# A decoder layer on one core: each gate's two 16-bit parts become one 32-bit word in the one-hot product, with four one-hot buffers and new gather rates

## The chip, the cores and the metric

The kernel runs on one core of a Trainium2 chip. The metric is device time in microseconds, from launch to end. Before the change three runs took 1726.3 to 1732.9 us, with a median of 1727.87 us. The profile is of one further execution.

The core's engines run side by side, each through its own list of instructions in fixed order, and wait for each other by semaphores: PE (TensorE, matmuls; PEld is its loading of weights), DVE (VectorE), ACT (ScalarE), POOL (GpSimd, which here issues the indirect DMAs that gather rows) and SP (SyncE, which issues the other DMAs). Sixteen DMA engines move the data between HBM and the on-chip memory.

## The reference, cut to what matters

The layer is one inference step for 512 prompt tokens and 64 sample tokens with the same weights: a projection, windowed attention and a spatial gating unit side by side, a merge, then a mixer over single-neuron experts (PEER), then a per-layer embedding. The change is in the mixer:

```python
q = (xb @ w_q).reshape(blk, PEER_HEADS, 2, PEER_HALF)
sc = jnp.einsum('thcd,hcnd->thcn', q, sub_keys)
s_top, i_top = lax.top_k(sc, PEER_TOPK)
...
best, pos = lax.top_k(cand, PEER_TOPK)
idx = jnp.take_along_axis(cand_idx, pos, axis=-1)
gate = jax.nn.softmax(best, axis=-1)
u = expert_u[idx]
act = jax.nn.gelu(jnp.einsum('thkd,td->thk', u, xb))
w = gate * act
return jnp.einsum('thk,thkd->td', w, expert_v[idx])
```

Each token takes 8 heads x 16 = 128 of the 16384 experts. An expert's number is i x 128 + j, with i from the first list of keys and j from the second.

## The kernel before, in words

**Two ways through the mixer.** 192 tokens (the 64 sample tokens and the first 128 prompt tokens, "tile" 0 and 1) are done by gathering: for each of 64 + 128 slots GpSimd fetches one row of `peer_u` per partition (L724, one indirect DMA of 128 rows of 4 KB), DVE forms the dot products (L736); then as many rows of `peer_v` are fetched and DVE adds them, weighted, to an accumulator (L743). That makes 192 + 192 row gathers, with five row buffers. The other 384 tokens (three tiles) are done densely over all experts, in blocks of 128 experts with the same j:

- *Stage 1* (`stage1`, 128 blocks): load a block of `peer_u` (512 KB), split it into a high and a low part (ACT L70, DVE L71 `w_lo`), 24 matmuls of 384 columns (`tform`, L86), GELU on ACT (L794). Each result is kept on chip, or spilled to HBM and read back.
- *G* (`build_g`): the gates as a dense matrix, for 16 tokens per call, 24 calls. For a token with chosen pairs (i, j) and gates g, G[i, j] is the sum of onehot(i) x (g onehot(j)) over its 128 choices, so a matmul of two one-hot matrices per token makes it. It goes to HBM (`gd`, 1 MB per call) and is read back by blocks.
- *Stage 2* (`stage2`, 128 blocks): multiply a block's activations by its part of G (DVE L1067), split the product and a block of `peer_v`, 18 matmuls of 512 columns (L1028) into six accumulators.

**How G is made before the change.** `make_ew` turns the lists of a tile so that the 128 choices lie on the partitions: `ij` holds i and j as f16. The gate, times 2^14, is kept as two f16 numbers, a high part and the rest (`g16`), and as the same two numbers in f32 (`gf`). `build_g` goes by groups of four tokens, 96 groups in all. DVE writes the one-hots of i and j for the four tokens in one operation (`hot`, L875, 128x1024 f16). Then onehot(j) is multiplied by both parts of the gate (`og`): in every even group ACT does it with 8 instructions of 128x128, one per token and part, with the gate's column as scale (L881); in every odd group DVE does it with 2 instructions of 128x512 (L887). PE then runs 8 matmuls, one per token and part, the two parts adding up in PSUM (L894), and ACT copies the four results into `gs` (L898). `hot` and `og` have three buffers (`OPB`); `gs` has two; after four groups SP writes `gs` to `gd` (L901).

**What sets the order.** Everything is recorded in program order and a scheduler sorts each engine's list by priorities; G's matmuls have a raised priority (`RUNP`). The program loops over the 24 calls of `build_g`, with as many stage-1 blocks between them as a goal line says; the top-16 selection of the last two tiles (`retrieve`) is worked off in the first seven (`TBK`). After the loop six more stage-1 blocks stand before the second stage. The second stage loops over j = 0 to 127 and runs one remaining stage-1 block at most steps until none are left.

**Gathers by credit.** `pay(x)` adds x to a credit and records one gather step for each whole unit. The rates are: `GT` per call of `build_g` (2.0 in the first seven calls, 3.5 in those behind, none in the last two), `GP` per stage-1 block (0.5 before the loop over G, 0 in it, 1.65 in the second stage), and `G2` per step of the second stage (1.6 while stage-1 blocks are left, 2.0 after that). At j = 122 (`TAIL1`) whatever is left is recorded at once. Before j = 126 the accumulator of the last gathered tile is read for its norm (L1014).

In this document the *middle stage* is the time from 572 us, about when DVE writes the first one-hots, to 852.57 us, when the first matmul of the second stage runs.

Of the kernel before, what the change touches and what calls it, by code (L numbers as in the profile page):

```python
# [18 lines left out]
P = 128  # L19
# [5 lines left out]
NJ = 128  # L25
TB = 16
JB = 8
GP = [0.5, 0.0, 1.65]
G2 = (1.6, 2.0)
SPILL = set(range(2, 40, 2))  # L30
NSP = len(SPILL)
GT = (2.0, 3.5)
GS = 2.0 ** 14
TAIL0 = 112
TAIL1 = 122
S1_TOPK = (4, 9, 13)
TBK = 7
S1_END = 6
OPB = 3
G_LAG = 3  # L40
RUNP = 400
RING = 44
# [9 lines left out]
def tile_decoder_step(ctx: ExitStack, tc: tile.TileContext, a, o):  # L52
    nc = tc.nc
    V, A, T, G, S = nc.vector, nc.scalar, nc.tensor, nc.gpsimd, nc.sync

    def pool(stack, name, bufs, side="left", **kw):
        return stack.enter_context(tc.tile_pool(name=name, bufs=bufs, side=side, reuse_waits="tile", **kw))
# [115 lines left out]
    for k in range(KC):  # L173
        with tc.high_priority(offset=1500):
            A.activation(xn[0][k], xT[k], AF.Copy, scale=vecs[:, k:k + 1])
            V.scalar_tensor_tensor(xn[1][k], xT[k], vecs[:, k:k + 1], xn[0][k].bitcast(F32),
                                   op0=ALU.mult, op1=ALU.subtract)
# [405 lines left out]
        split(xc, xn2[0][:, k, :], xn2[1][:, k, :])  # L583

    TOPK = ((4, 4), (0, 8), (1, 8), (2, 8), (3, 8))
    top = [tk.tile([P, 2, 8, 16], F32, name="top", bufs=5) for _ in TOPK]
    tix = [tk.tile([P, 2, 8, 16], U32, name="tix", bufs=5) for _ in TOPK]
    scs = []

    def key_scores(h, c, qp, sk):  # L590
# [139 lines left out]
    def gather_steps():  # L730
        for ti, ns in ((0, NS), (1, P)):
            dots = gp.tile([P, P], F32, name="dots")
            wts = gp.tile([P, P], F32, name="wts")
            for s in range(ns):
                row_ = gather_row(a["peer_u"], ixs[ti][:, s:s + 1])
                V.scalar_tensor_tensor(row_, row_, 1.0, xrs[ti], op0=ALU.mult, op1=ALU.mult,  # L736
                                       accum_out=dots[:, s:s + 1])
                yield
            A.activation(wts[:, :ns], dots[:, :ns], AF.Gelu_apprx_tanh)
            V.tensor_tensor(wts[:, :ns], wts[:, :ns], gts[ti][:, :ns], op=ALU.mult)  # L740
            for s in range(ns):
                row_ = gather_row(a["peer_v"], ixs[ti][:, s:s + 1])
                V.scalar_tensor_tensor(accs[ti], row_, wts[:, s:s + 1], accs[ti], op0=ALU.mult, op1=ALU.add)  # L743
                yield

    prev = None
# [53 lines left out]
    def make_ew(e0, e1_, gtf):  # L800
        pt = bank("pt")
        for q, src in enumerate((e0, e1_, gtf)):
            T.transpose(out=pt[:, q * P:(q + 1) * P], in_=src, identity=ident)
        ij = ep.tile([P, P // 2, 2, 2], F16, name="ij")
        g16 = ep.tile([P, P // 2, 2, 2], F16, name="g16")
        gf = ep.tile([P, 2, P], F32, name="gf")

        def halves(x):
            return x.rearrange("p (u t) -> p u t", t=2)

        for q in range(2):
            A.activation(ij[:, :, q, :], halves(pt[:, q * P:(q + 1) * P]), AF.Copy)
        A.activation(g16[:, :, 0, :], halves(pt[:, 2 * P:3 * P]), AF.Copy, scale=GS)
        A.activation(halves(gf[:, 0, :]), g16[:, :, 0, :], AF.Copy)
        V.scalar_tensor_tensor(gf[:, 1, :], pt[:, 2 * P:3 * P], GS, gf[:, 0, :], op0=ALU.mult, op1=ALU.subtract)
        A.activation(g16[:, :, 1, :], halves(gf[:, 1, :]), AF.Copy)
        ewT.append((ij, g16, gf))

    found = {}
    tqs.close()  # L820
# [40 lines left out]

    def build_g(tb):
        ti, t0 = divmod(tb * TB, P)
        ij, g16, gf = ewT[ti]
        gs = gsp[(tb + 1) % 2].tile([P, NJ, TB], F32, name="gs")
        for t4 in range(0, TB, 4):
            pt = psB.tile([P, 512], F32, name=("sc", "pt")[t4 // 4 % 2])
            hot = op.tile([P, 2, 2, P, 2], F16, name="hot")
            og = op.tile([P, 8 * P], F16, name="og")
            u0 = (t0 + t4) // 2  # L870

            def wide(x):
                return x.rearrange("p u f t -> p (u f) t")[:, :, None, :].to_broadcast([P, 4, P, 2])

            V.tensor_tensor(hot.rearrange("p u f j t -> p (u f) j t"), iota[:, None].to_broadcast([P, 4, P, 2]),  # L875
                            wide(ij[:, u0:u0 + 2]), op=ALU.is_equal)
            if t4 // 4 % 2 == 0:
                right = og.rearrange("p (t h j) -> p t h j", t=4, h=2)
                for t in range(4):
                    for h in range(2):  # L880
                        last = A.activation(right[:, t, h, :], hot[:, t // 2, 1, :, t % 2], AF.Copy,  # L881
                                            scale=gf[:, h, t0 + t4 + t:t0 + t4 + t + 1])
                pairs = [[(hot[:, t // 2, 0, :, t % 2], right[:, t, h, :]) for h in range(2)] for t in range(4)]
            else:
                right = og.rearrange("p (u h j t) -> p u h j t", u=2, h=2, t=2)
                for u in range(2):
                    last = V.tensor_tensor(right[:, u], hot[:, u, 1:2].to_broadcast([P, 2, P, 2]),  # L887
                                           g16[:, u0 + u][:, :, None, :].to_broadcast([P, 2, P, 2]), op=ALU.mult)
                pairs = [[(hot[:, t // 2, 0, :, t % 2], right[:, t // 2, h, :, t % 2]) for h in range(2)]
                         for t in range(4)]  # L890
            with tc.high_priority(offset=RUNP):
                for t in range(4):
                    for h in range(2):
                        g_last[tb] = T.matmul(pt[:, t * P:(t + 1) * P], lhsT=pairs[t][h][0], rhs=pairs[t][h][1],  # L894
                                              start=h == 0, stop=h == 1)
                        if t == h == 0:
                            after(g_last[tb], last)
                A.activation(gs[:, :, t4:t4 + 4], pt.rearrange("p (t j) -> p j t", t=4), AF.Copy, scale=1.0 / GS)  # L898
        if tb == NB // TB - 1:
            A.activation(g0, gs[:, 0:JB, :], AF.Copy)  # L900
        S.dma_start(gd[:, :, tb].rearrange("c p j t -> p c (j t)"), gs.rearrange("p (c j) t -> p c (j t)", j=JB))  # L901
# [13 lines left out]
    for g_ in (ples, xrs_):  # L915
        for _ in g_:
            pass
    pls.close()
    gs_s = ExitStack()
    ep = pool(gs_s, "ep", 2)  # L920
    op = pool(gs_s, "op", OPB)
# [110 lines left out]
    for j in range(NJ):  # L1032
        for jb in (2, 4) if j == 0 else (j + 4,):
            if jb in SPILL:
                back[jb] = d3.tile([P, NB], F32, name="x1c")
                S.dma_start(back[jb], ad[sorted(SPILL).index(jb)])
        if j and j - 1 not in SPILL and j1 < NJ:
            stage1()
        pay(G2[0] if j1 < NJ else G2[1])
        if j == TAIL0:  # L1040
            aLs.close()
            xds.close()
            spp.append(pool(sps, "spare", 2, "right"))
            gather(max(0, P - done[0]), mark_pe[0])
            pg = gp.tile([P, D], F32, name="xr")
            S.dma_start(pg, a["ple_g"])
            tails.append(gathered(0))
            for t in range(NB // P):
                x1s.append(spp[0].tile([P, D], F32, name="x1r", bufs=3))
                S.dma_start(x1s[t], x1r[t])  # L1050
        if j == TAIL1:
            gather(1000, mark_pe[0])
        if j == NJ - 2:
            tails.append(gathered(1))
        if j % JB == 0:
# [11 lines left out]
        V.tensor_tensor(wfv, wfv, gsl[:, :, j % JB, :], op=ALU.mult)  # L1067
# [158 lines left out]
```

## Time and profile before

| | |
|---|---|
| Median of three runs (lowest, highest) | 1727.87 us (1726.3, 1732.9) |
| The profiled execution's own time | 1727.91 us |
| Its span, first to last instruction | 1726.1 us |
| Mean granted clock of TensorE | 0.991 |
| PE, PEld busy | 1686.8, 1523.5 us |
| DVE, ACT, POOL busy | 1419.7, 843.2, 523.4 us |
| DMA, mean over the span | 266 GB/s, 459.11 MB |

How to read it: times count from the start of the span. In the view of 40 slices each digit is the busy share of a slice of 43 us in tenths. In windows and groups, "x" is a count of instructions, and a granted clock of 1.00 is full speed. The DMA share is the mean busy share of the 16 DMA engines, and can go a little over 1. A row of a group ends with the engine's idle time just before such instructions and what ended it. Matmuls overlap, so the time of one is longer than the distance from one to the next; an instruction of DVE or ACT, too, can begin some tens of ns before the one ahead of it ends. SPq and POOLq are the queues from which DMAs are issued.

### The profile page before, as it was taken

What the parts mean: (1) busy time and instruction counts of PE and PEld (TensorE: products, weight loads), DVE (VectorE), ACT (ScalarE), POOL (GpSimd) and SP (SyncE); (2) the same over time, 40 slices, a digit from 0 to 9 for tenths busy, and PEclk for the clock granted to TensorE, in tenths of its full rate; (3) what the DMA queues carried; (4) which work ended last, traced back from release to release, by engine and by line L of the source; (5) the groups of instructions that cost most, each with busy time, mean ns of one, the idle gap of its engine ahead of it and who ended that gap; (6) DMA issues with size and microseconds to landing.
All of it is one profiled execution on the core that took longest, in us unless ns stands there. A gap on an engine that the chain in (4) does not pass through costs nothing.

```text
span 1726.1 us, 27552 instructions
## 1 busy us (share of the span) xinstructions
PE 1686.8 (98%) x10040; PEld 1523.5 (88%) x10040; DVE 1419.7 (82%) x2788; ACT 843.2 (49%) x1528; POOL 523.4 (30%) x390
## 2 busy tenths in 40 slices
PE   8999999999999999888999999999999999999998
PEld 8988999999988999788888888898889998888877
DVE  7365666569899999999698899989888988999873
ACT  6566442343256899888633333333333333333352
POOL 0000000000001113445164555455544554566400
PEclk9999999999999999999999999999999999999999
DMA  6311222433257788999999999999999999999842
GB/s 236 97 62 50 74 95 100 154 102 97 82 165 265 242 278 292 382 357 358 338 355 356 373 401 411 392 396 390 371 339 349 362 345 322 342 375 374 318 165 79
DMA packets 179480, 459.11 MB, mean 266 GB/s; under 512 B 15505, under 2 KB 78993, under 8 KB 177297
## 3 DMA queue, kind: packets, MB, share of 16 engines
q1 hardware_dynamic: 123760, 255.29, 42.0%
q0 software_dynamic: 55584, 202.07, 31.2%
q8 instruction: 78, 1.28, 0.3%
q14 instruction: 58, 0.47, 0.1%
HBM read 420.67 MB, written 37.36 MB: 265 GB/s over the span
## 4 chain that ended last, share of the span: by engine, by line
PE 83%; DVE 11%; DMA 2%; ACT 2%; issue 1%; SPq 0%; ACTq 0%; DVEq 0%
PE mm L86 38%; PE oacc L1028 31%; PE pv L86 4%; DVE w_lo L71 2%; PE oacc L989 2%; PE sc L86 1%; DVE hot L875 1%; DVE row L736 1%; DMA gd<-gs 1%; PE pt L894 1%; PE mm L989 1%; DVE og L887 1%; PE sc L894 1%; ACT w_hi L70 1%; PE pv L338 1%
## 5 line engine op out<-in xcount | busy, mean ns | idle before, releaser
L70 ACT ACTIVATE w_hi<-w_raw 128x1024 fp32r<-128x1024 f32 x321 | 340.0, 1059 | 366.7 <-PE mm L86 278.7
L724 POOL DMA_INDIRECT row<-peer_u,idx x192 | 252.3, 1314 | 821.4 <-DVE best L641 471.4
L71 DVE TENSOR_TENSOR w_lo<-w_raw,w_hi 128x1024 fp32r<-128x1024 f32 x321 | 391.7, 1220 | 73.0 <-ACT w_hi L70 72.3
L86 PE MATMUL mm<-xd,w_hi 128*128 128x384 f32 x1552 | 407.2, 341 | 0.0
L724 POOL DMA_INDIRECT row<-peer_v,idx x192 | 269.6, 1404 | 237.9 <-DVE acc L743 212.7
L86 PE MATMUL mm<-x,w_hi 128*128 128x320 f32 (+1 forms) x1504 | 308.1, 299 | 0.0
L86 PEld LDWEIGHTS mm<-xd,w_hi 128*128 128x128 f32 x1552 | 286.1, 191 | 6.6 <-issue 0.2
L86 PE MATMUL mm<-xd,w_lo 128*128 128x384 f32 x776 | 263.7, 340 | 0.0
L86 PEld LDWEIGHTS mm<-x,w_hi 128*128 128x128 f32 x1504 | 241.8, 190 | 8.2 <-issue 7.4
L743 DVE SCALAR_TENSOR_TENSOR acc<-row,wts,acc 128x1024 f32<-128x1024 f32 x192 | 245.6, 1279 | 3.9 <-DMA row<-peer_v,idx 3.6
L736 DVE SCALAR_TENSOR_TENSOR row<-row,xr 128x1024 f32<-128x1024 f32 x192 | 232.6, 1218 | 13.3 <-DMA row<-peer_u,idx 13.3
L1028 PE MATMUL oacc<-w_hi,wh 128*128 128x512 f32 x768 | 241.3, 394 | 0.6 <-ACT wh L70 0.6
L1028 PE MATMUL oacc<-w_hi,wl 128*128 128x512 f32 x768 | 241.3, 395 | 0.3 <-DVE wl L71 0.3
L1028 PE MATMUL oacc<-w_lo,wh 128*128 128x512 f32 x768 | 240.8, 394 | 0.0
L86 PE MATMUL mm<-x,w_lo 128*128 128x320 f32 (+1 forms) x752 | 223.1, 297 | 0.0
L1028 PEld LDWEIGHTS oacc<-w_hi,wl 128*128 128x128 f32 x768 | 143.5, 187 | 36.6 <-DVE wl L71 1.2
L1028 PEld LDWEIGHTS oacc<-w_lo,wh 128*128 128x128 f32 x768 | 143.6, 187 | 35.4
L1028 PEld LDWEIGHTS oacc<-w_hi,wh 128*128 128x128 f32 x768 | 142.9, 187 | 30.4 <-ACT wh L70 1.0
L86 PEld LDWEIGHTS mm<-xd,w_lo 128*128 128x128 f32 x776 | 147.9, 191 | 0.1
L86 PEld LDWEIGHTS mm<-x,w_lo 128*128 128x128 f32 x752 | 142.4, 189 | 1.0 <-issue 0.8
L86 PE MATMUL pv<-xd,w_hi 128*128 128x384 f32 x496 | 132.1, 341 | 0.0
L881 ACT ACTIVATE og<-hot,gf 128x128 f16<-128x128 f16 x384 | 121.4, 393 | 4.8 <-DVE hot L875 4.8
(333 smaller groups left out, 2093.4 us busy)
## 6 DMA issues: line engine op xcount, KB each, us to landing
w_raw<-peer_uT SPq DMA_DIRECT2D x128, 512.0 KB, 6.1
w_raw<-peer_v SPq DMA_DIRECT2D x128, 512.0 KB, 6.7
gd<-gs SPq DMA_DIRECT2D x24, 1024.0 KB, 9.3
gs<-gd SPq DMA_DIRECT2D x15, 1536.0 KB, 9.9
w_raw<-w_in SPq DMA_DIRECT2D x30, 512.0 KB, 3.7
w_raw<-peer_wq SPq DMA_DIRECT2D x16, 512.0 KB, 3.6
w_raw<-w_br SPq DMA_DIRECT2D x8, 512.0 KB, 3.6
w_raw<-w_out SPq DMA_DIRECT2D x8, 512.0 KB, 3.5
```

The costliest lines, as they stand in the source:

```text
L70: A.activation(hi, src, AF.Copy)
L71: V.tensor_sub(lo, src, hi.bitcast(F32))
L86: mark_pe[0] = T.matmul(ps, lhsT=w[wi][:, wk + k, :], rhs=x[xi][k], start=i == 0, stop=i == n - 1)
L338: ins = T.matmul(pvs[pr, :], lhsT=vt[:, t0 + j, pr], rhs=pT, start=j == 0, stop=j == nj - 1)
L724: ins = G.indirect_dma_start(out=row_, out_offset=None, in_=table, in_offset=bass.IndirectOffsetOnAxis(ap=ix, axis=0))
L736: V.scalar_tensor_tensor(row_, row_, 1.0, xrs[ti], op0=ALU.mult, op1=ALU.mult, accum_out=dots[:, s:s + 1])
L743: V.scalar_tensor_tensor(accs[ti], row_, wts[:, s:s + 1], accs[ti], op0=ALU.mult, op1=ALU.add)
L875: V.tensor_tensor(hot.rearrange("p u f j t -> p (u f) j t"), iota[:, None].to_broadcast([P, 4, P, 2]), wide(ij[:, u0:u0 + 2]), op=ALU.is_e ...
L881: last = A.activation(right[:, t, h, :], hot[:, t // 2, 1, :, t % 2], AF.Copy, scale=gf[:, h, t0 + t4 + t:t0 + t4 + t + 1])
L894: g_last[tb] = T.matmul(pt[:, t * P:(t + 1) * P], lhsT=pairs[t][h][0], rhs=pairs[t][h][1], start=h == 0, stop=h == 1)
L989: T.matmul(p[:r, :hs.stop - hs.start], lhsT=xi[:, k, :r], rhs=w[k][wi][:, hs], start=k == 0 and xi is xh and wi == 0, stop=k == KC - 1 and ...
L1028: mark_pe[0] = T.matmul(oacc[t][hh], lhsT=wi[:, ts], rhs=vi[:, hh * 512:(hh + 1) * 512], start=j == 0 and last == 0 and vi is vh, stop=j = ...
```

## The change

Three things change.

1. **One word per gate.** `make_ew` writes the gate's high part and the rest side by side as two f16 numbers (`gpk`), the high part in the upper half; it is kept at 2^-14 or above. Read as one f32 number, the pair is multiplied by onehot(j) in a single operation with f32 output (`og`): 1 times the word is the word, 0 times it is 0. PE then reads the product as f16 again, every second element for one part. A group on ACT now takes 4 instructions of 128x128, a group on DVE takes 1 of 128x512. Which engine does a group changes too: in the first seven calls three of four groups go to ACT, behind that two of three. Counted in the built program, ACT has 264 such instructions for 384 and DVE 30 for 96. `make_ew` has three ACT instructions fewer per tile and one DVE instruction more.
2. **Four buffers.** `OPB` is 4. To make room, the top-16 lists of the first three tiles lie in a pool of their own that is closed before G's buffers are opened, and `wts` is computed in place in `dots`.
3. **Rates.** `GT` behind the seventh call is 2.9. `G2` has three values: 1.45 for j below 44, then 1.78 while stage-1 blocks are left, then 2.06.

```diff
-G2 = (1.6, 2.0)
+G2 = (1.45, 1.78, 2.06)
-GT = (2.0, 3.5)
+GT = (2.0, 2.9)
-OPB = 3
+OPB = 4
...
-        for q in range(2):
-            A.activation(ij[:, :, q, :], halves(pt[:, q * P:(q + 1) * P]), AF.Copy)
-        A.activation(g16[:, :, 0, :], halves(pt[:, 2 * P:3 * P]), AF.Copy, scale=GS)
-        A.activation(halves(gf[:, 0, :]), g16[:, :, 0, :], AF.Copy)
-        V.scalar_tensor_tensor(gf[:, 1, :], pt[:, 2 * P:3 * P], GS, gf[:, 0, :], op0=ALU.mult, op1=ALU.subtract)
-        A.activation(g16[:, :, 1, :], halves(gf[:, 1, :]), AF.Copy)
+        gpk = ep.tile([P, P, 2], F16, name="gpk")
+        for q in range(2):
+            A.activation(ij[:, :, q, :], pt[:, q * P:(q + 1) * P].rearrange("p (u t) -> p u t", t=2), AF.Copy)
+        V.tensor_scalar(gpk[:, :, 1], pt[:, 2 * P:3 * P], GS, 1.0 / GS, op0=ALU.mult, op1=ALU.max)
+        V.scalar_tensor_tensor(gpk[:, :, 0], pt[:, 2 * P:3 * P], GS, gpk[:, :, 1], op0=ALU.mult, op1=ALU.subtract)
...
-            og = op.tile([P, 8 * P], F16, name="og")
+            og = op.tile([P, 4, P], F32, name="og")
...
-            if t4 // 4 % 2 == 0:
-                right = og.rearrange("p (t h j) -> p t h j", t=4, h=2)
+            grp = tb * TB // 4 + t4 // 4
+            c = t0 + t4
+            if grp % 4 < 3 if tb < TBK else grp % 3 < 2:
                 for t in range(4):
-                    for h in range(2):
-                        last = A.activation(right[:, t, h, :], hot[:, t // 2, 1, :, t % 2], AF.Copy,
-                                            scale=gf[:, h, t0 + t4 + t:t0 + t4 + t + 1])
+                    last = A.activation(og[:, t, :], hot[:, t // 2, 1, :, t % 2], AF.Copy,
+                                        scale=gate[:, c + t:c + t + 1])
             else:
-                right = og.rearrange("p (u h j t) -> p u h j t", u=2, h=2, t=2)
-                for u in range(2):
-                    last = V.tensor_tensor(right[:, u], hot[:, u, 1:2].to_broadcast([P, 2, P, 2]),
-                                           g16[:, u0 + u][:, :, None, :].to_broadcast([P, 2, P, 2]), op=ALU.mult)
+                last = V.tensor_tensor(og.rearrange("p (u t) j -> p u t j", t=2),
+                                       hot[:, :, 1].rearrange("p u j t -> p u t j"),
+                                       gate[:, c:c + 4].rearrange("p (u t) -> p u t", t=2)[:, :, :, None]
+                                       .to_broadcast([P, 2, 2, P]), op=ALU.mult)
+            right = og.rearrange("p t j -> p (t j)").bitcast(F16).rearrange("p (t j h) -> p t j h", t=4, h=2)
...
-        pay(G2[0] if j1 < NJ else G2[1])
+        pay(G2[0 if j < 44 else 1 if j1 < NJ else 2])
```

What stands where in the built programs differs with it. The list of DVE in the middle stage, before the change, where the second dense tile's preparation ends and its first groups begin (`hot` is a one-hot operation, `og` a gate product, `row,dots` the dot products of a gathered row, `w_lo` the split of a stage-1 block):

```order
1119 L815 SCALAR_TENSOR_TENSOR gf<-pt,gf 128x128
1120 L875 TENSOR_TENSOR hot<-iota,ij 128x1024 x2
1121 L887 TENSOR_TENSOR og<-hot,g_6993 128x512 x2
1122 L736 SCALAR_TENSOR_TENSOR row,dots<-row,xr 128x1024
1123 L71 TENSOR_TENSOR w_lo<-w_raw,w_hi 128x1024
1124 L875 TENSOR_TENSOR hot<-iota,ij 128x1024
1125 L736 SCALAR_TENSOR_TENSOR row,dots<-row,xr 128x1024
1126 L887 TENSOR_TENSOR og<-hot,g_6993 128x512 x2
1127 L736 SCALAR_TENSOR_TENSOR row,dots<-row,xr 128x1024
1128 L875 TENSOR_TENSOR hot<-iota,ij 128x1024 x3
1129 L71 TENSOR_TENSOR w_lo<-w_raw,w_hi 128x1024
1130 L887 TENSOR_TENSOR og<-hot,g_6993 128x512 x2
```

The same place of DVE's list in the changed program, where the preparation has two instructions (`gpk`):

```order
1107 L809 TENSOR_SCALAR gpk<-pt 128x128
1108 L870 TENSOR_TENSOR hot<-iota,ij 128x1024
1109 L810 SCALAR_TENSOR_TENSOR gpk<-pt,gpk 128x128
1110 L737 SCALAR_TENSOR_TENSOR row,dots<-row,xr 128x1024
1111 L870 TENSOR_TENSOR hot<-iota,ij 128x1024
1112 L71 TENSOR_TENSOR w_lo<-w_raw,w_hi 128x1024
1113 L879 TENSOR_TENSOR og<-hot,gpk 128x512
1114 L870 TENSOR_TENSOR hot<-iota,ij 128x1024
1115 L737 SCALAR_TENSOR_TENSOR row,dots<-row,xr 128x1024
1116 L870 TENSOR_TENSOR hot<-iota,ij 128x1024
1117 L737 SCALAR_TENSOR_TENSOR row,dots<-row,xr 128x1024
1118 L879 TENSOR_TENSOR og<-hot,gpk 128x512
```

A pair of products for every second one-hot has become one product for two or three one-hots. Over the whole middle stage DVE's list holds 66 gathered rows between the first and the last one-hot before, and 56 now.

The end of the gathers in DVE's list, before the change (`acc` adds a row of `peer_v`, `wl` and `w_lo` are the splits for one step of the second stage):

```order
1950 L743 SCALAR_TENSOR_TENSOR acc<-row,wts,acc 128x1024
1951 L71 TENSOR_TENSOR wl<-x_5421,wh 128x384
1952 L743 SCALAR_TENSOR_TENSOR acc<-row,wts,acc 128x1024
1953 L71 TENSOR_TENSOR w_lo<-w_raw,w_hi 128x1024
1954 L71 TENSOR_TENSOR wl<-x_5421,wh 128x384
1955 L71 TENSOR_TENSOR w_lo<-w_raw,w_hi 128x1024
```

And in the changed program:

```order
1939 L744 SCALAR_TENSOR_TENSOR acc<-row,dots,acc 128x1024
1940 L71 TENSOR_TENSOR w_lo<-w_raw,w_hi 128x1024
1941 L71 TENSOR_TENSOR wl<-aL,wh 128x384
1942 L71 TENSOR_TENSOR w_lo<-w_raw,w_hi 128x1024
1943 L71 TENSOR_TENSOR wl<-aL,wh 128x384
1944 L71 TENSOR_TENSOR w_lo<-w_raw,w_hi 128x1024
```

The last gather stood seven splits of `peer_v` (`w_lo`) before the end of the second stage, and stands three before it now.

More of the change, by code (lines that the diff above doesn't have):

```diff
@@ L585, in tile_decoder_step @@
     TOPK = ((4, 4), (0, 8), (1, 8), (2, 8), (3, 8))
-    top = [tk.tile([P, 2, 8, 16], F32, name="top", bufs=5) for _ in TOPK]
-    tix = [tk.tile([P, 2, 8, 16], U32, name="tix", bufs=5) for _ in TOPK]
+    tes = ExitStack()
+    te = pool(tes, "te", 1, "right")
+    top = [pl.tile([P, 2, 8, 16], F32, name="top", bufs=n) for pl, n in ((te, 3),) * 3 + ((tk, 2),) * 2]
+    tix = [pl.tile([P, 2, 8, 16], U32, name="tix", bufs=n) for pl, n in ((te, 3),) * 3 + ((tk, 2),) * 2]
     scs = []
@@ L732, in gather_steps @@
             dots = gp.tile([P, P], F32, name="dots")
-            wts = gp.tile([P, P], F32, name="wts")
             for s in range(ns):
@@ L738, in gather_steps @@
                 yield
-            A.activation(wts[:, :ns], dots[:, :ns], AF.Gelu_apprx_tanh)
-            V.tensor_tensor(wts[:, :ns], wts[:, :ns], gts[ti][:, :ns], op=ALU.mult)
+            A.activation(dots[:, :ns], dots[:, :ns], AF.Gelu_apprx_tanh)
+            V.tensor_tensor(dots[:, :ns], dots[:, :ns], gts[ti][:, :ns], op=ALU.mult)
             for s in range(ns):
                 row_ = gather_row(a["peer_v"], ixs[ti][:, s:s + 1])
-                V.scalar_tensor_tensor(accs[ti], row_, wts[:, s:s + 1], accs[ti], op0=ALU.mult, op1=ALU.add)
+                V.scalar_tensor_tensor(accs[ti], row_, dots[:, s:s + 1], accs[ti], op0=ALU.mult, op1=ALU.add)
                 yield
@@ L804, in make_ew @@
         ij = ep.tile([P, P // 2, 2, 2], F16, name="ij")
[L805 to L809, printed above, removed]
+        gpk = ep.tile([P, P, 2], F16, name="gpk")
         for q in range(2):
-            A.activation(ij[:, :, q, :], halves(pt[:, q * P:(q + 1) * P]), AF.Copy)
-        A.activation(g16[:, :, 0, :], halves(pt[:, 2 * P:3 * P]), AF.Copy, scale=GS)
-        A.activation(halves(gf[:, 0, :]), g16[:, :, 0, :], AF.Copy)
-        V.scalar_tensor_tensor(gf[:, 1, :], pt[:, 2 * P:3 * P], GS, gf[:, 0, :], op0=ALU.mult, op1=ALU.subtract)
-        A.activation(g16[:, :, 1, :], halves(gf[:, 1, :]), AF.Copy)
-        ewT.append((ij, g16, gf))
+            A.activation(ij[:, :, q, :], pt[:, q * P:(q + 1) * P].rearrange("p (u t) -> p u t", t=2), AF.Copy)
+        V.tensor_scalar(gpk[:, :, 1], pt[:, 2 * P:3 * P], GS, 1.0 / GS, op0=ALU.mult, op1=ALU.max)
+        V.scalar_tensor_tensor(gpk[:, :, 0], pt[:, 2 * P:3 * P], GS, gpk[:, :, 1], op0=ALU.mult, op1=ALU.subtract)
+        ewT.append((ij, gpk))
     found = {}
@@ L863, in build_g @@
         ti, t0 = divmod(tb * TB, P)
-        ij, g16, gf = ewT[ti]
+        ij, gpk = ewT[ti]
+        gate = gpk.rearrange("p t h -> p (t h)").bitcast(F32)
         gs = gsp[(tb + 1) % 2].tile([P, NJ, TB], F32, name="gs")
@@ L876, in build_g @@
                             wide(ij[:, u0:u0 + 2]), op=ALU.is_equal)
-            if t4 // 4 % 2 == 0:
-                right = og.rearrange("p (t h j) -> p t h j", t=4, h=2)
+            grp = tb * TB // 4 + t4 // 4
+            c = t0 + t4
+            if grp % 4 < 3 if tb < TBK else grp % 3 < 2:
                 for t in range(4):
-                    for h in range(2):
-                        last = A.activation(right[:, t, h, :], hot[:, t // 2, 1, :, t % 2], AF.Copy,
-                                            scale=gf[:, h, t0 + t4 + t:t0 + t4 + t + 1])
-                pairs = [[(hot[:, t // 2, 0, :, t % 2], right[:, t, h, :]) for h in range(2)] for t in range(4)]
-            else:
-                right = og.rearrange("p (u h j t) -> p u h j t", u=2, h=2, t=2)
-                for u in range(2):
-                    last = V.tensor_tensor(right[:, u], hot[:, u, 1:2].to_broadcast([P, 2, P, 2]),
-                                           g16[:, u0 + u][:, :, None, :].to_broadcast([P, 2, P, 2]), op=ALU.mult)
-                pairs = [[(hot[:, t // 2, 0, :, t % 2], right[:, t // 2, h, :, t % 2]) for h in range(2)]
-                         for t in range(4)]
+                    last = A.activation(og[:, t, :], hot[:, t // 2, 1, :, t % 2], AF.Copy,
+                                        scale=gate[:, c + t:c + t + 1])
+            else:
+                last = V.tensor_tensor(og.rearrange("p (u t) j -> p u t j", t=2),
[3 more added lines that the diff above has]
+            right = og.rearrange("p t j -> p (t j)").bitcast(F16).rearrange("p (t j h) -> p t j h", t=4, h=2)
             with tc.high_priority(offset=RUNP):
@@ L893, in build_g @@
                     for h in range(2):
-                        g_last[tb] = T.matmul(pt[:, t * P:(t + 1) * P], lhsT=pairs[t][h][0], rhs=pairs[t][h][1],
-                                              start=h == 0, stop=h == 1)
+                        g_last[tb] = T.matmul(pt[:, t * P:(t + 1) * P], lhsT=hot[:, t // 2, 0, :, t % 2],
+                                              rhs=right[:, t, :, 1 - h], start=h == 0, stop=h == 1)
                         if t == h == 0:
@@ L918, in tile_decoder_step @@
     pls.close()
+    tes.close()
     gs_s = ExitStack()
```

## The prediction

> **What bounds the kernel now.** I read the page first, then the windows by stage, the waits of the middle stage, its groups of instructions, its DMA table, and last the chain. The page, in 40 slices:
>
> ```profile
> span 1726.1 us, 27552 instructions
> PE   8999999999999999888999999999999999999998
> DVE  7365666569899999999698899989888988999873
> DMA  6311222433257788999999999999999999999842
> ```
>
> PE (TensorE) looks full everywhere, but a busy matmul is not a matmul at its peak, so I went by stage (columns: length, then busy time and count of PE, PEld, DVE, ACT, POOL, then granted clock, DMA share, GB/s):
>
> ```profile
> 572.00:676.00 104.00, 102.96 (x740) 96.58 (x739) 103.76 (x248) 95.81 (x220) 21.55 (x16) 1.00 0.82 261
> 676.00:836.00 160.00, 142.64 (x1076) 130.91 (x1075) 145.94 (x248) 142.25 (x374) 68.83 (x51) 0.94 1.04 364
> 852.00:1662.00 810.00, 809.68 (x3869) 702.97 (x3868) 722.54 (x896) 292.92 (x393) 420.32 (x308) 1.00 0.95 360
> ...
> 572.00:852.57 280.57, 261.20 (x1900) 242.25 (x1898) 256.07 (x501) 245.80 (x606) 90.38 (x67) 0.96 0.95 324
> ```
>
> The change lives in the middle stage, where G is built between stage-1 blocks: from about 572 us to the first matmul of the second stage at 852.57, 280.6 us. In the second stage PE is busy 809.68 of 810 us at full clock, and the chain shows its pace:
>
> ```profile
> 836.24 5.84 DMA gd<-gs
> 842.17 7.68 DMA gs<-gd
> 852.57 3.52 PE oacc L1028 x14
> ...
> 862.58 4.18 PE mm L86 x24
> 866.75 8.40 PE oacc L1028 x36
> ```
>
> A stage-1 matmul passes in 4.18/24 = 0.174 us and nothing waits: no work of the other engines that hides there can shorten it. In the middle stage the matmuls number (the stage-1 line, then G's line, each alone in the window):
>
> ```profile
> 572.00:852.57 280.57, 223.40 (x1121) 197.59 (x1119) 0.96 0.95 324
> ...
> 572.00:852.57 280.57, 65.22 (x768) 46.75 (x768) 0.96 0.95 324
> ...
> 712.38 0.91 PEld L894 LDWEIGHTS <-hot 128*128 128x128 f16 x16 [0.16 <-DVE og L887]
> ```
>
> That is 1121 x 0.174 = 195.2 us, and 768 x 0.91/16 = 43.7 us: 239 us of PE work in 280.6. So about 41 us are idle or slow time, and that is all this stage can give. Who causes it (engine, line, what it waited for: total, times, longest):
>
> ```profile
> POOL row L724 <- DVE row L736: 134.3, 48, 15.1
> PEld L894 <- DVE og L887: 23.2, 36, 3.2
> PE pt L894 <- DVE og L887: 14.4, 12, 2.9
> ```
>
> PE waits 37.6 us for the DVE half of the gate products and almost nowhere else; GpSimd waits for DVE too. DVE is busy 256.1 of 280.6 us, 103.76 of 104 in the first part. The clock completes the picture:
>
> ```profile
> 750.00:760.00 10.00, 7.08 (x50) 6.51 (x50) 10.00 (x19) 8.68 (x25) 5.31 (x4) 0.73 1.03 358
> ```
>
> Where PE idles, the next matmuls run at a lower grant: 0.94 over 676 to 836. **DVE bounds this stage, with ACT and the DMA engines (share 1.04) close behind.**
>
> **The change part by part.** The DVE and ACT groups of the middle stage (count, busy, mean ns):
>
> ```profile
> L736 DVE SCALAR_TENSOR_TENSOR row<-row,xr 128x1024 f32<-128x1024 f32 x60 | 72.3, 1215 | 0.0
> L71 DVE TENSOR_TENSOR w_lo<-w_raw,w_hi 128x1024 fp32r<-128x1024 f32 x45 | 54.9, 1220 | 11.5 <-ACT w_hi L70 11.4
> L887 DVE TENSOR_TENSOR og<-hot,g 128x512 f16<-128x512 f16 x96 | 36.9, 422 | 0.0
> L736 DVE DVE_READ_ACCUMULATOR row<-row,xr 128x1 f32 x60 | 4.8, 79 | 0.0
> ...
> L881 ACT ACTIVATE og<-hot,gf 128x128 f16<-128x128 f16 x384 | 121.4, 393 | 4.8 <-DVE hot L875 4.8
> L814 ACT ACTIVATE gf<-g 128x128 f32<-128x128 f16 x3 | 0.9, 307 | 0.0
> ...
> L1067 DVE TENSOR_TENSOR x<-x,gs x66: 547/552/559, 849.9 to 1460.1; 128x384 f32<-128x384 f32 x66
> ```
>
> *The gate product on DVE.* Before, 96 products of 36.9 us. After, 30 groups go to DVE, one 128x512 product each with a 32-bit output and one 32-bit input. No row shows that mix. Lower bound: the 16-bit product of the same size, 422 ns. Upper: 32-bit products take 552 ns at 384 columns and 1220 at 1024, 1.044 ns per column, hence 552 + 128 x 1.044 = 686 ns at 512. I take 686, since two of three operands are 32-bit: 30 x 0.686 = 20.6 us. DVE saves 16.3 us (24 at the lower bound).
>
> *The gate product on ACT.* 384 instructions become 264 (66 groups x 4). Their pace is 121.4/384 = 0.316 us each. The new ones write f32 and take an f32 column as scale; the nearest row is L814, f16 to f32 over 128 columns, 307 ns against 393: no sign that a 32-bit output costs more. 120 x 0.316 = 37.9 us saved, and three small copies per tile fall away (9 x 0.3 = 2.6 us). One more DVE instruction per tile in the preparation costs 3 x 0.3 = 0.9 us.
>
> *The matmuls of G* keep their number and shape; the right operand is now always read with a gap of one element, which the DVE half already did: cost 0.
>
> *The gathers.* A row gathered costs DVE 1.215 + 0.079 = 1.29 us. The order has 66 of them among the one-hots of the middle stage before and 56 after: 12.9 us of DVE leave the stage, and so do ten transfers:
>
> ```profile
> q1 hardware_dynamic: 58787, 55.42, 60.7%
> q0 software_dynamic: 9648, 35.13, 34.1%
> ...
> row<-peer_u,idx POOLq DMA_INDIRECT x55, 7.2
> ...
> row<-peer_v,idx POOLq DMA_INDIRECT x12, 7.9
> ```
>
> 67 gathers took 34.1% of 280.6 us, 1.43 us of all 16 DMA engines each: 14.3 us less.
>
> *Sum for the middle stage.* DVE: 256.1 - 16.3 + 0.9 - 12.9 = 227.8, that is 28.3 us less; with the 24.5 us in which it idled before, 252. ACT: 245.8 - 40.5 = 205. PE: 239 at best. DMA: 60.7 + 34.1 + 0.4% of 280.6 = 267 us of work, less 14.3; if its mean share stays at 0.95, the stage shrinks by 14.3/0.952 = 15.0 us. So 28.3 us if DVE sets the pace to the end, 15.0 if the DMA engines take over. I take the middle, 21.5: PE becomes the first engine, but the DMA share is already 1.04 in the second part.
>
> [...] I go by the trace: short gaps that go give the clock back, up to 0.06 x 160 = 9.6 us, which is part of the 41.
>
> *Four one-hot buffers.* DVE waited for G's matmuls to free one only 6.4 us in all by this row; a part of that goes and is inside the 28.
>
> ```profile
> DVE hot L875 <- PE sc L894: 6.4, 4, 2.4
> ```
>
> *The second stage.* Ten gathers more, at 1.43 us of DMA and 1.28 of DVE. They lie beside PE: DVE is busy 722.5 of 810 us, and would be 735. The rate falls from 1.6 to 1.45 per step up to j = 43, rises to 1.78 until stage 1 is used up and to 2.06 behind that. The tight place is the last:
>
> ```profile
> 1500.00:1600.00 100.00, 100.00 (x430) 80.17 (x429) 97.32 (x96) 36.18 (x48) 69.00 (x48) 1.00 1.00 373
> ...
> 1630.72 1.28 DVE L743 SCALAR_TENSOR_TENSOR acc<-row,wts,acc 128x1024 f32<-128x1024 f32 x1
> ...
> 1656.32 1.04 ACT L1014 ACTIVATE xn<-xr 64x1024 f32<-64x1024 f32 x1
> ```
>
> A step there is half of 8.40 us, DVE leaves 2.7% of it, 0.11 us, and 0.06 gathers x 1.28 = 0.08 us are added: it just fits; about 20 such steps would cost 1.5 us if it did not. I charge those 1.5. The last accumulation moves three to four steps later by the order, to about 1647, before its reader at 1656: no cost.
>
> Sum: the profiled execution took 1727.9 us, 1.8 around its span, and equals the median of the runs (1727.87). 1727.9 - 21.5 + 1.5 = **1707.9 us**.
>
> **The rivals.**
>
> *The DMA engines are the bound, in both stages* (chance 0.18). Then the middle stage gives 15.0 and the second stage takes the moved 14.3 back: 1727.2 us, no change. For it: share 1.04 in the second part, 0.95 behind. Against it: the waits of 572 to 842 name no engine that waits for a gather or a weight, and in the second stage PE loses 0.3 of 810 us. [...]
>
> *PE comes close to its floor* (0.18). If with ACT's shorter product, evenly spread groups and full clock only 6 us of the 41 remain, the gain is 35: 1692.9 us. For it: PE's waits have one cause. Against it: three engines within 5% of each other, in a fixed order.
>
> *ACT becomes the bound: slower* (0.09). If an ACT product with 32-bit scale and output costs more than the 16-bit one, 66 of 96 groups now stand on the wrong engine. ACT without any products has 245.8 - 121.4 - 2.6 = 121.8 us; it fills the whole 280.6 from (280.6 - 121.8)/264 = 0.60 us per instruction. At 0.65 the stage takes 293: 1727.9 + 12.8 = 1740.7 us. L814's 307 ns speaks against it, but L814 has no column as scale.
>
> That the product isn't halved can't be: the order has 264 and 30 product instructions where there were 384 and 96.
>
> **How the numbers follow.** Forecast 0.55, its gain between 10 and 28 us; DMA 0.18; PE's floor 0.18; ACT 0.09. About 0.5%, 8.6 us, can be told from no change: faster 0.55 + 0.18 = 0.73, same 0.18, slower 0.09. The range leaves out ACT's case and half of the PE-floor case: 1692 to 1727.
>
> **What would show it.** Right: L881's successor at about 0.32 us and L887's at 0.69; PE's wait for the DVE product below 15 us; the clock from 676 on back near 1.00; the second stage beginning near 831 and taking some 810 us. Wrong: ACT above 95% of the stage; ACT or DVE waiting for rows, weights or the write of G; idle PE between 860 and 1660.

## The result and the profile after

Five runs of the changed kernel took 1711.17 to 1717.06 us, median 1715.17; five of the kernel before, on the same chip, 1726.3 to 1732.9, median 1728.18. The ratio is 0.9916, 95% interval 0.9897 to 0.9936: 14.5 us faster, where 20 had been forecast. The profiled execution took 1715.17 us, its span 1713.3, 12.8 us less than before.

The windows of the kernel after, with the columns of those before (length, busy of PE, PEld, DVE, ACT, POOL, clock, DMA share, GB/s), by stage; the last row is its middle stage, which now ends at 837.45:

```profile
572.00:676.00 104.00, 103.37 (x767) 95.93 (x766) 102.38 (x233) 92.45 (x202) 19.89 (x15) 1.00 0.84 263
676.00:836.00 160.00, 148.55 (x1115) 138.59 (x1114) 129.45 (x197) 115.73 (x272) 56.25 (x42) 0.97 1.02 361
852.00:1662.00 810.00, 808.98 (x3868) 701.26 (x3867) 731.45 (x899) 300.14 (x412) 442.91 (x315) 1.00 0.97 363
...
572.00:837.45 265.45, 253.37 (x1888) 235.96 (x1887) 233.27 (x432) 208.28 (x475) 76.14 (x57) 0.98 0.95 322
```

The gain is in the middle stage: 265.5 us for 280.6. DVE and ACT are no longer full there. From its end to the end of the span it is 875.85 us for 873.53, of which ten stage-1 matmuls that now stand behind the border are 1.7 us. (The border of before, 852.57, is where the chain first meets the second stage. Four of its matmuls had run from 851.0 on and PE had then waited; in the changed kernel the first one runs at 837.3. From first matmul to first matmul the gain of the middle stage is 13.7 us.)

The groups of the middle stage that answer to those shown of before (count, busy, mean ns, idle before):

```profile
L737 DVE SCALAR_TENSOR_TENSOR row<-row,xr 128x1024 f32<-128x1024 f32 x57 | 68.6, 1217 | 0.2 <-DMA row<-peer_u,idx 0.2
L71 DVE TENSOR_TENSOR w_lo<-w_raw,w_hi 128x1024 fp32r<-128x1024 f32 x46 | 56.1, 1219 | 25.7 <-ACT w_hi L70 25.4
L879 DVE TENSOR_TENSOR og<-hot,gpk 128x512 f32<-128x512 f16 x30 | 20.5, 684 | 0.0
...
L876 ACT ACTIVATE og<-hot,gpk 128x128 f32<-128x128 f16 x264 | 86.1, 395 | 6.3 <-DVE hot L870 6.3
```

The two new products cost what the prediction said, 684 ns on DVE and 86.1/264 = 0.326 us on ACT. The idle column of `w_lo` says that DVE now waits 25.4 us for ACT, where before it was 11.4; but 14.7 us of it are three waits that end after G's last matmuls (816 us), from where on PE is full. The waits of the kernel after, 572 to 838 us, say for what ACT stands:

```profile
DVE w_lo L71 <- ACT w_hi L70: 25.4, 8, 9.1
...
PEld L887 <- issue: 21.7, 64, 4.8
ACT gs L891 <- DMA gd<-gs: 13.5, 5, 5.2
...
PE pt L887 <- ACT og L876: 7.3, 4, 4.7
...
PEld L887 <- DVE og L879: 2.9, 16, 0.3
```

PE's 37.6 us for DVE's products have become 3.1. Its waits for ACT's products went from 3.3 to 11.5 us, and those to which the profile gives no releaser ("issue") from 9.5 to 21.7. ACT waits 13.5 us, before 2.3, until a write of G to HBM (`gd<-gs`) has landed and given its buffer back. ACT works in order, so the products and splits behind that copy wait too, and with them DVE and PE. One such place, in order of time (in brackets the idle time before, and what ended it):

```profile
698.78 0.60 ACT L891 ACTIVATE gs<-sc 128x512 f32<-128x512 f32 x1 [5.21 <-DMA gd<-gs]
700.36 1.23 DVE L71 TENSOR_TENSOR w_lo<-w_raw,w_hi 128x1024 fp32r<-128x1024 f32 x1 [4.79 <-ACT w_hi L70]
701.05 0.37 PE L887 MATMUL pt<-og,hot 128*128 128x128 f16 x2 [4.70 <-ACT og L876]
701.05 0.21 PEld L887 LDWEIGHTS <-hot 128*128 128x128 f16 x2 [4.76 <-issue]
```

The longest of the waits without a releaser, 4.76 us, is thus PE's wait for a product that stands behind such a copy. The chain of the kernel after shows the writes one by one (start, length):

```profile
660.05 8.56 DMA gd<-gs
...
685.61 13.07 DMA gd<-gs
...
735.81 14.47 DMA gd<-gs
...
798.59 10.50 DMA gd<-gs
```

And its windows show PE short of work, and its clock down, at or just behind them:

```profile
680.00:700.00 20.00, 16.35 (x124) 15.38 (x123) 15.57 (x26) 11.72 (x28) 8.65 (x7) 0.96 1.04 383
700.00:720.00 20.00, 18.95 (x138) 17.44 (x137) 17.89 (x26) 15.15 (x39) 6.64 (x5) 0.87 1.01 336
...
800.00:820.00 20.00, 15.82 (x120) 14.29 (x120) 7.29 (x10) 12.20 (x31) 0.00 (x0) 0.91 0.85 277
```

**Theory A**: DVE was the bound, and once it is relieved the write of G is the next one: 1 MB per call, two buffers, DMA engines that are busy with gathers and weights (share 1.02 from 676 to 836 us). **Rivals**: the gain is simply DVE's relief in part (B), or what is left above PE's work is the fixed order and the latency from ACT to PE and back (C).

### The profile page after: what moved, and what is told of

The parts are those of the page before. It is cut to its first block, busy times and chain, and to the rows that moved or that the text cites. A ratio compares the mean times of both kernels' runs of the same rounds, so it can differ in the third digit from the quotient of the medians.

```text
span 1713.3 us, 27406 instructions
## 1 busy us (share of the span) xinstructions
PE 1680.2 (98%) x10040; PEld 1518.4 (89%) x10040; DVE 1406.5 (82%) x2725; ACT 806.9 (47%) x1399; POOL 536.2 (31%) x390
## 4 chain that ended last, share of the span: by engine, by line
PE 86%; DVE 6%; DMA 4%; ACT 3%; issue 1%; SPq 0%; ACTq 0%; DVEq 0%
PE mm L86 40%; PE oacc L1022 31%; PE pv L86 4%; DMA gd<-gs 3%; PE oacc L983 2%; DVE w_lo L71 1%; PE sc L86 1%; PE pt L887 1%; ACT w_hi L70 1%; PE mm L983 1%; PE sc L887 1%; PE sc L596 1%; PE pv L338 1%; ACT og L876 0%; DMA w_raw<-peer_uT 0%
## 5 line engine op out<-in xcount | busy, mean ns | idle before, releaser
L726 POOL DMA_INDIRECT row<-peer_u,idx x192 | 262.8, 1369 | 812.5 <-PE pv L86 470.3
L86 PE MATMUL mm<-xd,w_hi 128*128 128x384 f32 x1552 | 401.6, 337 | 0.0
L86 PEld LDWEIGHTS mm<-xd,w_hi 128*128 128x128 f32 x1552 | 282.0, 188 | 6.5
L744 DVE SCALAR_TENSOR_TENSOR acc<-row,dots,acc 128x1024 f32<-128x1024 f32 x192 | 245.4, 1278 | 4.8 <-DMA row<-peer_v,idx 4.6
L1022 PEld LDWEIGHTS oacc<-w_hi,wh 128*128 128x128 f32 x768 | 143.0, 187 | 29.4
L70 ACT ACTIVATE wh<-x 128x384 fp32r<-128x384 f32 x66 | 34.6, 525 | 166.0 <-PE oacc L1022 165.9
```

The source lines that it names most:

```text
L70: A.activation(hi, src, AF.Copy)
L86: mark_pe[0] = T.matmul(ps, lhsT=w[wi][:, wk + k, :], rhs=x[xi][k], start=i == 0, stop=i == n - 1)
L726: ins = G.indirect_dma_start(out=row_, out_offset=None, in_=table, in_offset=bass.IndirectOffsetOnAxis(ap=ix, axis=0))
L744: V.scalar_tensor_tensor(accs[ti], row_, dots[:, s:s + 1], accs[ti], op0=ALU.mult, op1=ALU.add)
L1022: mark_pe[0] = T.matmul(oacc[t][hh], lhsT=wi[:, ts], rhs=vi[:, hh * 512:(hh + 1) * 512], start=j == 0 and last == 0 and vi is vh, stop=j = ...
```

## The experiments

Each result is a ratio to the kernel before, run in turns on the same chip; "below" is 1 less that ratio, times 1728 us. Medians of the kernel before were 1728 to 1731 in the four sittings.

### The parts by themselves

Four runs take the change apart. The word alone: the changed kernel with

```diff
-G2 = (1.45, 1.78, 2.06)
-GT = (2.0, 2.9)
-OPB = 4
+G2 = (1.6, 1.6, 2.0)
+GT = (2.0, 3.5)
+OPB = 3
```

> The one-word product alone, with three one-hot buffers and the gather rates of before. Theory A (the G write): once DVE is relieved, the write of G through two buffers, on DMA engines that are busy all the time, sets the pace of the middle stage; with all 66 gathers still in it, the relief of DVE (16 us) buys little: 1722 to 1727 us, and ACT's copies wait for the write of G by over 10 us. Theory B (DVE's share): the gain of 13 us splits as DVE's relief does, 16.3 of 28.3 us by the product: about 1720.5 us, with few waits for the write.

The rates alone: the kernel before with the new `G2`, `GT` and the line that picks `G2`.

> The new gather rates alone, in the kernel of before. Theory A: ten gathers fewer relieve DVE by 12.9 us and the DMA engines by 14.3 us at once, and DVE stays the bound: 8 to 12 us faster, 1716 to 1720. Theory B: 12.9 of 28.3 parts of 13 us, about 1722.

The word and the fourth buffer: the changed kernel with the old `G2` and `GT`.

> The changed kernel with the gather rates of before (one word, four buffers). Theory A: as the one-word product alone, 1722 to 1727 us, since a fourth one-hot buffer does nothing for the write of G. Theory B: about 1720. If buffers matter by themselves, this is over 3 us faster than the run with three.

The word and the rates: the changed kernel with `OPB = 3`.

> The changed kernel with three one-hot buffers instead of four. Theory A: within 2 us of the changed kernel, 1713 to 1717, since one-hots wait for a buffer only 2.8 us. Rival: the fourth buffer lets DVE and ACT run ahead of PE and is worth 4 us or more: 1719 or slower.

| run | ratio (95%) | below before |
|---|---|---|
| word alone | 0.9939 (0.9925 to 0.9953) | 10.5 us |
| rates alone | 0.9940 (0.9924 to 0.9957) | 10.4 us |
| word, four buffers | 0.9949 (0.9935 to 0.9963) | 8.8 us |
| word, rates | 0.9901 (0.9887 to 0.9916) | 17.1 us |
| all three (the change) | 0.9916 (0.9897 to 0.9936) | 14.5 us |

The fourth one-hot buffer is worth nothing that shows: with and without it agree within their intervals, twice (with three, and the new rates, the kernel came out 2 us below what was expected). The word alone gained more than either theory said, though ACT does wait 10.9 us for the write there, as A had it; with the fourth buffer its time is that of theory B. The rates alone came out as theory A said. Neither is a share of the whole, as B has it: 10.5 and 10.4 make 20.9 alone and 14.5 to 17.1 together. Something both run into seems to take 4 to 6 us of it; each gain is uncertain by 2.4 to 3.4 us, so this is only just more than the noise.

### The write of G

A third buffer for G's results. Memory for it comes from the other buffers: three for one-hots and two for products, where the changed kernel has four of each.

```diff
-OPB = 4
+OPB = 2
...
-            hot = op.tile([P, 2, 2, P, 2], F16, name="hot")
+            hot = op.tile([P, 2, 2, P, 2], F16, name="hot", bufs=3)
...
-    gsp = [pool(gs_s, "gsp%d" % i, 1) for i in range(2)]
+    gsp = [pool(gs_s, "gsp%d" % i, 1) for i in range(3)]
...
-        gs = gsp[(tb + 1) % 2].tile([P, NJ, TB], F32, name="gs")
+        gs = gsp[(tb + 1) % 3].tile([P, NJ, TB], F32, name="gs")
```

> The changed kernel with a third buffer for G's results (gs), paid for in memory by the product buffers, of which two are left; the one-hots have three. The bytes that move stay the same. Theory A, as a matter of buffers: ACT no longer waits for the write of G, and of the 27 us that the middle stage still has above its matmuls 8 to 15 go: 22 to 30 us below the kernel before. Theory A, as a matter of DMA work: a third buffer only lets one write more stand in the queue, 0 to 4 us of gain: 13 to 18 below before. Rival C (order and latency): the writes' waits are covered by others, two product buffers cost a little: 10 to 15 below before.

Half of the write: only the first 8 of 16 chunks of G go to HBM, and the second stage reads them twice.

```diff
-        S.dma_start(gd[:, :, tb].rearrange("c p j t -> p c (j t)"), gs.rearrange("p (c j) t -> p c (j t)", j=JB))
+        S.dma_start(gd[:8, :, tb].rearrange("c p j t -> p c (j t)"),
+                    gs.rearrange("p (c j) t -> p c (j t)", j=JB)[:, :8])
...
-                S.dma_start(gsl[:, :nb], gd[j // JB][:, :nb])
+                S.dma_start(gsl[:, :nb], gd[j // JB % 8][:, :nb])
```

> The changed kernel, in which only half of G is written to HBM and the second stage reads that half twice: the other half of G is left out of the computation. 12 MB less in the middle stage, all else alike. Theory A: the waits for the write fall from 13.5 us to below 3 and the middle stage loses 10 to 18 us more: 23 to 32 us below before. Rival C: under 5 us more, 13 to 19 below before.

No gathers in the middle stage: `GT = (0.0, 0.0)`, and 8 of the first tile's 64 dot products are left.

> The changed kernel without any gathers in the middle stage: 56 of the 64 dot products of the first gathered tile are left out, the second stage keeps its gathers. DVE loses some 70 us and the DMA engines some 80 us of work there. Theory A: writes of G land in about 6 us, no wait for them is left, PE comes within 8 us of its 239 us: 30 to 35 us below before. Rival C (fixed order, chain of ACT, PE and the copies): at most 20 us below before.

Fewer gathers in the middle stage, all of them done later: `GT = (2.0, 1.9)`, `G2 = (1.65, 1.9, 2.06)`.

> The changed kernel with 15 more gathers moved from the middle to the second stage (1.9 per call for 2.9, then 1.65, 1.9 and 2.06 per step). Theory A: 21 us less DMA work in the middle stage, 8 to 14 us gained there; the second stage hides them as it hid the ten: 21 to 28 us below before. If the second stage can't hide them (DVE at 93% of it), PE waits behind 1000 us and the kernel is no faster than the changed one or slower: 5 to 15 below before.

| run | ratio (95%) | below before | second stage begins |
|---|---|---|---|
| third gs buffer | 0.9845 (0.9821 to 0.9869) | 26.8 us | 829.9 |
| half of the write | 0.9830 (0.9808 to 0.9853) | 29.4 us | 821.2 |
| no gathers there | 0.9829 (0.9806 to 0.9852) | 29.5 us | 820.5 |
| 15 gathers moved | 1.0010 (0.9994 to 1.0026) | -1.7 us | 843.8 |

The third buffer moves the same bytes and still gains 10 to 12 us over the change: rival C falls as the whole of the explanation, and the wait is one of buffers at least in part. The nearest kernel with two buffers is the word with the rates, which has three one-hot buffers too, and as good as the same order at the end: 108 stage-1 matmuls stand between G's last group and the second stage, 109 with the third buffer. The waits and the DMA tables (median time from issue to landing, 676 to 820 us) of these two, first with two buffers, then with three:

```profile
ACT gs L891 <- DMA gd<-gs: 18.7, 9, 4.0
...
gd<-gs SPq DMA_DIRECT2D x16, 1024.0 KB, 12.5
```

```profile
ACT gs L891 <- DMA gd<-gs: 4.7, 2, 3.3
...
gd<-gs SPq DMA_DIRECT2D x16, 1024.0 KB, 12.9
```

A write takes as long in both, longer than in the kernel before, where it was 10.4 in the same window; with three buffers ACT waits 4.7 us for it, with two 18.7. (The profiled run with three, 1708.1 us, is the slowest of its five.) Without gathers on the DMA engines the same megabyte lands in half the time:

```profile
gd<-gs SPq DMA_DIRECT2D x13, 1024.0 KB, 6.1
```

That run came within half a microsecond of the least that was expected of it. It takes some 70 us off DVE as well, so it doesn't tell the two apart; the halved write, 8.1 us to landing and 2.5 us of waits, does as much with DVE's work unchanged.

The fourth run refutes what I had made of theory A, that less DMA work is enough: 21 us of it less, and the gain of the change is gone. Its profiled execution is 16.2 us longer than the changed kernel's: 6.3 us in the middle stage and 9.9 behind it, or 8.4 and 7.8 with the twelve stage-1 matmuls more that stand behind the border put back. So about half of the loss is the second stage's, the other case that was expected: PE waits 6.2 us there for DVE's split `wl`. The waits of this run in the middle stage, PE in the stage's second part, and the writes on its chain:

```profile
ACT gs L891 <- DMA gd<-gs: 19.5, 7, 4.5
ACT gs L1055 <- DMA gd<-gs: 7.8, 1, 7.8
```

```profile
676.00:836.00 160.00, 143.00 (x1052) 132.28 (x1051) 113.25 (x170) 109.28 (x264) 30.93 (x26) 0.95 0.92 310
```

```profile
678.91 11.64 DMA gd<-gs
...
698.04 12.85 DMA gd<-gs
...
731.37 11.03 DMA gd<-gs
...
757.31 8.46 DMA gd<-gs
...
773.01 9.78 DMA gd<-gs
...
794.44 13.97 DMA gd<-gs
```

The DMA share is only 0.92, and a write lands in 9.5 us (median), yet ACT waits 19.5 us for writes among G's copies and 7.8 more before the second stage's first block, which takes one of the same two buffers; writes are 40% of the chain from 676 to 845. With fewer gathers in DVE's list the order asks for the calls of G sooner: the last write is issued at 794 us, in the changed kernel at 817, while 273 stage-1 matmuls are left behind G's last group, for 122. Where nothing holds them, writes are issued 5 to 9 us apart; with two buffers the next call but one can't begin to copy before the first has landed. PE idles at G's groups, and the stage-1 work that could have filled the gap stands behind them. So theory A in its new form: **the fixed order asks for G faster than two buffers can be written.** A write landed in 6.1 us where the DMA share was 0.75 (no gathers there), in 9.5 us at 0.92 here and in 12.9 us at 1.05 (third buffer); the waits come at 0.92 too.

### The new form, and the split

The same rates as in the fourth run, with three gs buffers:

> Three buffers for gs with 15 more gathers moved to the second stage, which with two buffers was 2 us slower than before. Theory A in its new form (a fixed order that asks for G faster than two buffers can be written): the third buffer takes the waits for the write from 27 us to below 8, and what is left of the loss is the second stage's 6 to 8 us: 15 to 24 below before. If the loss of that run came from elsewhere (the second stage, the order of PE), the third buffer changes little: 0 to 8 below before.

Rates between those (`GT = (2.0, 2.4)`, `G2 = (1.55, 1.83, 2.06)`), three gs buffers:

> Three buffers for gs with 7 to 8 more gathers moved (2.4 per call, then 1.55, 1.83 and 2.06 per step). Theory A in its new form: as with the rates of the change or a little better, 24 to 31 below before. If every gather moved now costs the second stage as much as it gives: 20 to 26 below before.

The old rates, three gs buffers:

> Three buffers for gs (three for one-hots, two for products) with the gather rates of before. If the write's buffers were what held the one-word product back, it now shows its own gain without the rates: 18 to 24 us below before, 3 to 9 less than with the new rates, because DVE has 12.9 us more to do. If the rates did their work through the DMA engines and the third buffer makes that needless: 24 to 29 below, as with the new rates.

The changed kernel with the products dealt out as before:

```diff
-            if grp % 4 < 3 if tb < TBK else grp % 3 < 2:
+            if grp % 2 == 0:
```

> The changed kernel with the products dealt out as before, every second group on ACT and every second on DVE: DVE has 18 products more (12.3 us), ACT 72 instructions fewer (23 us). If DVE's relief is used up once the write of G is the bound: 12 to 16 below before, as the changed kernel. If DVE still counts one for one: 4 to 8 below before.

| run | ratio (95%) | below before |
|---|---|---|
| 15 gathers moved, three gs buffers | 0.9881 (0.9865 to 0.9897) | 20.6 us |
| 7 to 8 gathers moved, three gs buffers | 0.9850 (0.9834 to 0.9867) | 25.9 us |
| old rates, three gs buffers | 0.9930 (0.9913 to 0.9947) | 12.1 us |
| every second group on ACT | 0.9868 (0.9851 to 0.9885) | 22.8 us |

The first bears out the new form for the fourth run above. One buffer more for G, one less for one-hots and two less for products, and 22 us are back, in the traces 25 in the middle stage and none behind it; ACT waits no longer for a write among G's copies; PE in the second part of the middle stage is full at full clock, and the second stage begins at 818.5 instead of 843.8:

```profile
676.00:836.00 160.00, 160.00 (x1201) 149.96 (x1199) 128.28 (x191) 122.17 (x285) 38.42 (x30) 1.00 1.00 341
```

The order of PE's list is another one, too: 173 stage-1 matmuls stand behind G's last group, not 273, so 100 of them, 17 us of PE's work, now stand before it. How much of the 25 us is the buffer itself and how much the order that comes with it, no run tells.

What it loses against the run with the rates of the change is in the second stage, where PE now waits for DVE:

```profile
PE oacc L1022 <- DVE wl L71: 8.0, 3, 6.0
```

So the second stage hides ten gathers more, and not 25. Seven or eight more, in between, are neither better nor worse than the rates of the change; both expectations allowed that.

The old rates with three buffers missed both expectations: 12.1 us, no more than the word alone gains with two, which the intervals don't tell apart. Its waits and its DMA rows:

```profile
ACT gs L891 <- DMA gd<-gs: 2.1, 1, 2.1
...
676.00:836.00 160.00, 152.15 (x1120) 139.44 (x1118) 138.20 (x205) 118.35 (x278) 74.76 (x51) 0.96 1.05 378
...
gd<-gs SPq DMA_DIRECT2D x15, 1024.0 KB, 14.8
```

The third buffer did its work here as well: among G's copies ACT waits 2.1 us for a write, where with two buffers it was 10.9, though a write needs 14.8 us. The kernel is no faster for it, so with 66 gathers the write's buffers are not what holds the stage, and theory A doesn't say what does. The DMA engines are at 1.05 of their time, DVE is busy 138 of 160 us, and with three buffers the new rates are worth 14.7 us, close to the 14.3 us of DMA work that the prediction had for the ten gathers. That points to the DMA engines; no run shows it. What is shown is that the third buffer pays only together with the rates.

The split missed both expectations as well: dealing every second group to each engine is 5 to 8 us *better* than the new split, by 0.9868 against 0.9901 and 0.9916. The 18 products given back to DVE cost nothing that shows; why there is a gain stays open. Products on ACT stand behind the copies that wait for the write, products on DVE don't, which would fit; but the profiled run was this kernel's slowest, 1712.3 us, and its trace doesn't tell. It wasn't tried with three gs buffers.

This run tells something more. Against the rates alone it has the same rates and deals the groups out the same way; what is new is the word (and the fourth buffer, which is worth nothing that shows). The products of the rates alone, then of this run:

```profile
L881 ACT ACTIVATE og<-hot,gf 128x128 f16<-128x128 f16 x384 | 122.5, 397 | 0.6 <-DVE hot L875 0.5
L887 DVE TENSOR_TENSOR og<-hot,g 128x512 f16<-128x512 f16 x96 | 37.2, 424 | 0.0
```

```profile
L876 ACT ACTIVATE og<-hot,gpk 128x128 f32<-128x128 f16 x192 | 63.0, 393 | 18.6 <-DVE hot L870 18.5
L879 DVE TENSOR_TENSOR og<-hot,gpk 128x512 f32<-128x512 f16 x48 | 32.8, 683 | 0.0
```

The word is worth 12.4 us here (0.9940 to 0.9868), and DVE's time for products falls by only 4.4 us; ACT's falls by 59.5. So DVE's lighter list can account for about a third of these 12 us, about half at the near end of the two intervals. ACT's lighter list, or the shorter way of a group to its product (four instructions of ACT for eight), may be; they were not tried apart.

## Why the prediction was right, and what was mis-sized

- **The bound.** Right in part. DVE's products were what PE waited for most: 37.6 us became 3.1, and the word, with hardly a byte moved, gains 10.5 us alone. But the prediction put the word's worth into 16.3 us of DVE's time, and the runs don't bear that out: with every second group on ACT, DVE has 12.3 of them back and the kernel is 6 to 8 us faster, and against the rates alone the word gains 12.4 us with 4.4 of DVE's. The new dealing of the groups, a part of the change, costs time. That DVE's total set the pace of the stage is not shown; ACT's list, a close second in the prediction, was relieved more.
- **The price of the two products.** 686 ns taken, 684 measured; 0.316 us taken on ACT, 0.326 measured. The rival in which ACT's 32-bit product makes the kernel slower is out, though ACT has more groups than is best.
- **The second stage.** 1.5 us were charged for the ten gathers that it takes over, 0.6 are left (2.3 less 1.7). Right, and shown to have an end: 25 gathers are not hidden.
- **The sum for the middle stage is the term that was mis-sized**: 21.5 us taken, 15.1 measured, 13.4 without the ten matmuls that changed sides (13.7 and 12.0 from first matmul to first matmul). I had asked which engine's total would set the pace, and put it between DVE's and the DMA engines'. With the changed kernel's rates none of the totals did. A wait that cost 2.3 us before took over: the two buffers of G's write. One of the prediction's signs of being wrong, ACT waiting for the write of G, is what came. Most of its price was in the trace: a write landed in 9.6 us (median, 676 to 840 us), and calls had been 8 to 12 us apart, mostly about 10. As an estimate, a second part 21 us shorter asks for a call every 8 to 9 us; with two buffers the call after the next can't copy before the write has landed. What the trace of before didn't have is that the write itself got slower: 12.5 us with the word and the rates, where it was 10.4 from 676 to 820 us before; why stays open. I had read the DMA engines' share and not the time a buffer is held.
- **15.0 us by the DMA engines' share** was a bound of the prediction and is nearly what came. That is luck and no proof of it: the third buffer moves as many bytes in 257.9 us, and with less DMA work and two buffers the stage grew. The range, 1692 to 1727 us, held the result because it was wide; no term of the sum foresaw what took the missing 6 us.
- **The rival "DMA in both stages"** was half right: the write landed later beside busier DMA engines (6.1 us at a share of 0.75, without gathers; 12.5 us at 1.01, word and rates), but the second stage did not give the ten gathers' time back.
- **PE's floor** (gain of 35) did not come, the write stood before it; with the write halved, or without gathers, the stage came within 12 to 14 us of the 235 to 237 us of the matmuls that then stood in it, where the changed kernel is 28 us above.
- **The fourth buffer** was given a part of the 28 us; it got nothing.
- **The clock** went from 0.94 to 0.97 in the second part, not to 1.00; PE idles 11.5 us there for 17.4, so two thirds of the gaps are still there, others than before.

The fastest versions that compute the whole layer were the changed kernel with a third gs buffer (0.9845) and the same with seven or eight gathers more moved (0.9850); they can't be told apart.

## What to carry to other kernels

When one engine's list is lightened, look next at every buffer that returns only when a transfer has landed, and compare landing time with the new distance between its uses; here a wait of 2.3 us in the old profile was the one that grew. In a fixed order, relief of one engine also changes how early others are asked for work, so moving more work out can make a stage longer (by 6.3 us here, with 15 gathers moved). Measure the parts of a change alone and together: sums that don't add up hint at a common bound behind them. And when a change lightens two engines' lists at once, vary the split between them: the engine that the waits name need not be the one whose relief pays (here PE's waits named DVE, and with 12.3 us of products given back to DVE the changed kernel was 6 to 8 us faster).

## What the hardware showed that was not expected

- A write of 1 MB in runs of 512 bytes landed in 6.1 us without gathers beside it, in 10.4 us in the kernel before and in 14.8 us at a DMA share of 1.05 (medians, 676 to 820 us). Half a megabyte beside gathers took 8.1 us. Here a transfer's length was set by its neighbours more than by its size.
- The DMA engines, at 364 GB/s and a share of 1.04 from 676 to 836 us in the kernel before, moved 378 GB/s in the same window at a share of 1.05 with the old rates and three gs buffers.
- A DVE product with one 16-bit and one 32-bit input and a 32-bit output takes 684 ns at 512 columns, the price of an all-32-bit one by the line through 552 and 1220 ns (686). On ACT an f32 output costs next to nothing over f16: 395 ns for 393.
